# New costs for the interleaving of u products with routing and gates, and a second search over 64 pairs

## The chip, the cores and the metric

One core of a Trainium2 chip runs the whole program. The metric is device time in microseconds (us). Five engines work side by side: PE multiplies matrices (PEld is its loading of weights), DVE and POOL work on vectors, ACT computes functions and copies with a change of type, SP issues most of the DMAs. Each engine takes its own instructions strictly in the order in which the program holds them; an instruction that waits holds back all that stand behind it on its engine.

## The reference

The program has two layers on 256 tokens of width 1024. Each layer is a mixer (s5 in the first, sparse attention in the second) and then an expert layer, and the change touches the expert layers alone. Cut to what matters:

```python
qk = (h @ w_q).reshape(b, s, 8, 2, 128)              # 8 heads, two halves each
sc = einsum('bshcd,hckd->bshck', qk, sub_keys)       # 128 keys in each half
s1, i1 = top_k(sc[..., 0, :], 16)
s2, i2 = top_k(sc[..., 1, :], 16)
cand = (s1[..., :, None] + s2[..., None, :])         # 16 x 16 sums of a head
top_s, top_pos = top_k(cand.reshape(..., 256), 16)   # 16 experts of a head
gates = softmax(top_s)
act = gelu(einsum('cd,ced->ce', h, u_tab[experts])) * gates
out = einsum('ce,ced->cd', act, v_tab[experts])
```

## The kernel before

No expert is gathered. The kernel multiplies h with all 128x128 rows of u, takes the gelu, multiplies by a dense table of gates (zero where an expert was not chosen) and multiplies with all rows of v. Activations stand transposed: features or experts on the partitions, the 256 tokens along the free axis. B, one buffer of 128 x 128 x 256, holds the activations of all experts of a layer.

A product of full precision is three matmuls: a weight is split into w_hi, written by ACT (L139), and w_lo, the rest, written by DVE (L181), in halves of 128x512 with four buffers each. A "u product" (function `U`) turns one 512 KB slab of u into 24 matmuls of 128x256 (L188, L189, L190; the last needs w_lo). 128 of them make a layer, two to a bank of PSUM; a bank leaves through ACT (gelu, L733, L736) and, where gates are there already, through a DVE product (L737).

An expert layer then has four stages, all on the same five engines:

- Route (`route_steps`): per head two products with w_q (`head`), the scores, `top16` on 128 scores four times (`topk1`) and on the 256 sums for each 128 tokens (`topk2`; L864 to L868, L907).
- Decode, twice, for 128 tokens t each: positions are turned into two indices (L920 to L923), in eight parts a comparison on DVE (L930) and a product on POOL (L932) and a sum on DVE (L935); then Exp on ACT (L938), sums, and a transposition into `slotT`.
- Gates (`G`): 64 turns q of four tokens. DVE writes two tables, oij (L761) and ohl (L764), two buffers each; PE makes eight matmuls of 128x128 into one bank (L769); DVE multiplies what is there of B with that bank (L772), ACT copies the rest (L775).
- v products (`VS`, L798): 128 turns; left-over u products and, in the first layer, steps of the second layer's modulation (`ada_steps`, L233) are dealt among them.

The order in which u products are mixed with routing, decoding and gates is set by `weave`: each step of the side work yields a pair of costs (PE, DVE) in us, each u product yields its own pair, and as long as the sum of DVE costs exceeds that of PE costs the next u product is taken. A scheduler then places instructions on each engine; in decoding and among v products DVE's order is that of the code. The numbers yielded are therefore what sets the order.

Of the kernel before, what the change touches and what calls it, by code (L numbers as in the profile page):

```python
# [10 lines left out]
F16 = mybir.dt.float16  # L11
I32 = mybir.dt.int32
U32 = mybir.dt.uint32
# [697 lines left out]
def peer_layer(K, layer, h):  # L711
    tc, nc = K.tc, K.nc
    V = nc.vector
    with tc.tile_pool(name=f"pr{layer}", bufs=1, reuse_waits="tile") as pp, \
            tc.tile_pool(name=f"pw{layer}", bufs=2, reuse_waits="tile") as wp, ExitStack() as es:

        B = pp.tile([P, NJ, S], F32, name="B")
        slotT = pp.tile([P, 2, S // 2, 2, 2], F16, name="slotT")
        done = [0]
        ugelu = [0]  # L720
        u_src, v_src = K.aps["peer_u"], K.aps["peer_v"]

        def U():

            late = []

            def evac():
                c, ps = late.pop()
                pv = ps.rearrange("p (j t) -> p j t", j=2)
                t0 = done[0]  # L730
                out = B[:, 2 * c:2 * c + 2]
                if t0 < S:
                    nc.scalar.activation(out[:, :, t0:], pv[:, :, t0:], AF.Gelu_apprx_tanh)  # L733
                if t0 > 0:
                    g = wp.tile([P, 2, S], F32, name="ge", bufs=1)
                    nc.scalar.activation(g[:, :, :t0], pv[:, :, :t0], AF.Gelu_apprx_tanh)  # L736
                    V.tensor_mul(out[:, :, :t0], g[:, :, :t0], out[:, :, :t0])  # L737
                ugelu[0] = 2 * c + 2
                return 0.6 if t0 else 0.0

            for c in range(NJ // 2):
                ps = bank(K)
                for m in range(2):
                    chunk_T(K, split_w(K, load_unit(K, u_src[layer, 2 * c + m])), h, ps[:, m * S:(m + 1) * S])
                    dve = evac() if late and m == 0 else 0.0
                    yield 2.62, U_DVE + dve
                late.append((c, ps))
            evac()
            yield 0.0, 0.6

        def G(gp):

            tab = K.iota2
            full = [P, 4, P, 2]
            for q in range(S // 4):
                ts = slice(4 * q, 4 * q + 4)

                oij, ohl = (gp.tile([P, 2, 2, P, 2], F16, name=n) for n in ("oij", "ohl"))
                si, sg = (slotT[:, n, 2 * q:2 * q + 2].rearrange("p a n t -> p (a n) t")[:, :, None, :].to_broadcast(full)
                          for n in range(2))  # L760
                V.tensor_tensor(oij.rearrange("p a n j t -> p (a n) j t"), tab[:, None].to_broadcast(full), si,  # L761
                                op=OP.is_equal)
                oj = oij[:, :, 1, None].to_broadcast([P, 2, 2, P, 2])
                V.tensor_tensor(ohl, oj, slotT[:, 1, 2 * q:2 * q + 2, :, None, :].to_broadcast([P, 2, 2, P, 2]), op=OP.mult)  # L764
                ps = bank(K)
                pv = ps.rearrange("p (j t) -> p j t", t=4)
                for t in range(4):
                    for n in range(2):
                        nc.tensor.matmul(pv[:, :, t], oij[:, t // 2, 0, :, t % 2], ohl[:, t // 2, n, :, t % 2],  # L769
                                         start=(n == 0), stop=(n == 1), skip_group_check=True)  # L770
                jd = ugelu[0]
                V.scalar_tensor_tensor(B[:, :jd, ts], pv[:, :jd], 1.0 / GS, B[:, :jd, ts],  # L772
                                       op0=OP.mult, op1=OP.mult)
                if jd < NJ:
                    nc.scalar.activation(B[:, jd:, ts], pv[:, jd:], AF.Copy, scale=1.0 / GS)  # L775
                done[0] = 4 * q + 4
                yield 0.5, 1.5

        u = U()
        weave(u, route_steps(K, layer, h, B, slotT))  # L780
        assert ugelu[0] <= ROUTE_J
        with tc.tile_pool(name=f"pg{layer}", bufs=2, reuse_waits="tile") as gp:
            weave(u, G(gp))
        acc = [[bank(K) for _ in range(2)] for _ in range(2)]

        vp = es.enter_context(tc.tile_pool(name=f"pv{layer}", bufs=2, reuse_waits="tile"))

        def VS():

            for j in range(NJ):  # L790
                raw = load_unit(K, v_src[layer, j])
                with tc.high_priority(offset=PRIO):
                    a = split(K, B[:, j], [P, S], "a", pool=vp)
                for dh, w in enumerate(split_w(K, raw)):
                    for t in range(2):
                        ts = slice(t * P, (t + 1) * P)
                        for al, wl in ((0, 0), (0, 1), (1, 0)):
                            nc.tensor.matmul(acc[t][dh], a[al][:, ts], w[wl],  # L798
                                             start=(j == 0 and al + wl == 0), stop=(j == NJ - 1 and al == 1))
                yield j  # L800

        ada = ada_steps(K, vp, ADA_T) if layer == 0 else iter(())
        with tc.manual_schedule(engines={mybir.EngineType.DVE, mybir.EngineType.SP}):
            credit = 0.0
            for j in VS():
                credit += 0.4 if next(u, None) is None else 0.8
                while credit >= 1.0:
                    next(ada, None)
                    credit -= 1.0
        assert next(u, None) is None  # L810
        for _ in ada:
            pass
    return acc
# [25 lines left out]


ROUTE_J = 64
U_DVE = 1.3


def route_steps(K, layer, h, B, slotT):
# [6 lines left out]
    qk = [cv([S]) for _ in range(4)]  # L852
    sc = [cv([2, 2, P]) for _ in range(3)]
    sc2 = [cv([P]) for _ in range(2)]
    cand = [cv([16, 16]) for _ in range(2)]
    cand2 = [cv([256]) for _ in range(2)]
    val = cv([2, H, 2, TK])
    idx = cv([2, H, 2, TK], U32)
    idf = cv([2, H, 2, TK])
    ts = cv([2, H, TK])  # L860
    pos = cv([2, H, TK], U32)

    def top16(v, i, src, tmp):
        V.max(v[:, 0:8], src)  # L864
# [15 lines left out]
    def head(u):  # L880
# [4 lines left out]
        for c in range(2):  # L885
# [7 lines left out]
            while len(late) > (3 if 2 * u + c < 3 else 0):  # L893
                scores()
            late.append((u, c, q, ps2))
            yield 2.8, 1.14

    def topk1(u):
        for c in range(2):
            for t in range(2):  # L900
                top16(val[:, t, u, c], idx[:, t, u, c], sc[u % 3][:, c, t], sc2[t])
                yield 0, 1.0

    def topk2(u):
        for t in range(2):
            cd = cand[t]
            V.tensor_add(cd, val[:, t, u, 0, :, None].to_broadcast([P, 16, 16]),  # L907
                         val[:, t, u, 1, None, :].to_broadcast([P, 16, 16]))
            top16(ts[:, t, u], pos[:, t, u], cd.rearrange("p a b -> p (a b)"), cand2[t])
            yield 0, 2.0  # L910

    def decode(t):
        cw = Carve(B.rearrange("p j t -> p (j t)"), ROUTE_J * S + t * 8192)
        ab = cw([2, H, TK], U32)
        abf = cw([2, H, TK])
        sel = cw([2, H, TK])
        eq = cw([2, H, TK, 16])
        e, z, el = cw([H, TK]), cw([H]), cw([H, TK])
        e16 = cw([H * TK // 2]).bitcast(F16).rearrange("p (h k) -> p h k", h=H)
        V.tensor_scalar(ab[:, 0], pos[:, t], 4, None, op0=OP.logical_shift_right)  # L920
        V.tensor_scalar(ab[:, 1], pos[:, t], 15, None, op0=OP.bitwise_and)
        V.tensor_copy(abf, ab)
        V.tensor_copy(idf[:, t], idx[:, t])  # L923
        yield 0, 1.2
        shape = [P, 2, TK, 16]
        parts = [(c, slice(2 * i, 2 * i + 2)) for i in range(4) for c in range(2)]
        for n in range(len(parts) + 2):
            if n < len(parts):
                c, hs = parts[n]
                V.tensor_tensor(eq[:, c, hs], abf[:, c, hs, :, None].to_broadcast(shape),  # L930
                                K.iota[:, None, None, 0:16].to_broadcast(shape), op=OP.is_equal)
                nc.gpsimd.tensor_mul(eq[:, c, hs], eq[:, c, hs], idf[:, t, hs, c, None, :].to_broadcast(shape))  # L932
            if n > 1:
                c, hs = parts[n - 2]
                V.tensor_reduce(sel[:, c, hs], eq[:, c, hs], axis=AX.X, op=OP.add)  # L935
            yield 0, 1.2
        V.tensor_sub(e, ts[:, t], ts[:, t, :, 0:1].to_broadcast([P, H, TK]))
        nc.scalar.activation(e, e, AF.Exp)  # L938
        V.tensor_reduce(z, e, axis=AX.X, op=OP.add)
        V.reciprocal(z, z)  # L940
        V.scalar_tensor_tensor(e, e, GS, z[:, :, None].to_broadcast([P, H, TK]), op0=OP.mult, op1=OP.mult)
# [12 lines left out]
    for u in range(9):  # L954
# [5 lines left out]
        if u > 0:  # L960
            yield from topk1(u - 1)
            yield from topk2(u - 1)
    with K.tc.manual_schedule(engines={mybir.EngineType.DVE}):
        for t in range(2):
            yield from decode(t)

# [450 lines left out]
```

## Time and profile before

| what | us |
|---|---|
| median of 3 runs | 2086.83 |
| lowest, highest | 2086.11, 2086.85 |
| profiled execution | 2087.91 |
| its span | 2086.1 |
| PE busy in the span | 2022.8 (97%) |
| DVE busy in the span | 1609.8 (77%) |
| ACT busy in the span | 1154.2 (55%) |
| POOL busy in the span | 113.6 (5%) |

The mean granted clock of TensorE is 0.986 of full speed. In time, the first layer routes from about 212 to 345 us, decodes to 416, makes gates to 657 and v products to 1046; the second layer routes from 1240 to 1369, decodes to 1440, makes gates to 1680 and v products to 2070. A busy share is an average over these stages, so a stage has to be looked at by itself; a matmul's end is modelled, and a matmul that overlaps the one before it counts once.

### The profile page before, as it was taken

What the parts mean: (1) busy time and instruction counts of PE and PEld (TensorE: products, weight loads), DVE (VectorE), ACT (ScalarE), POOL (GpSimd) and SP (SyncE); (2) the same over time, 40 slices, a digit from 0 to 9 for tenths busy, and PEclk for the clock granted to TensorE, in tenths of its full rate; (3) what the DMA queues carried; (4) which work ended last, traced back from release to release, by engine and by line L of the source; (5) the groups of instructions that cost most, each with busy time, mean ns of one, the idle gap of its engine ahead of it and who ended that gap; (6) DMA issues with size and microseconds to landing.
All of it is one profiled execution on the core that took longest, in us unless ns stands there. A gap on an engine that the chain in (4) does not pass through costs nothing. (4 is left out here: it accounts for less than half of the span.)

```text
span 2086.1 us, 39288 instructions
## 1 busy us (share of the span) xinstructions
PE 2022.8 (97%) x14344; PEld 1840.6 (88%) x14344; DVE 1609.8 (77%) x3698; ACT 1154.2 (55%) x2396; POOL 113.6 (5%) x149
## 2 busy tenths in 40 slices
PE   6889999999999999999999999999999999999998
PEld 3778999899999988888888789999999998888887
DVE  9696899878887777777775869998788865556665
ACT  4775555555445555555555755555554455555554
POOL 4220001200000000000010000021000000000000
PEclk9899999999999999999999999999999999999998
DMA  7445555544445788888863045555444455666562
GB/s 285 147 180 162 162 172 172 157 151 139 142 142 177 259 277 267 271 268 270 276 228 112 22 141 163 172 165 163 138 142 142 142 173 189 194 192 193 193 195 95
DMA packets 102690, 377.18 MB, mean 181 GB/s; under 512 B 11488, under 2 KB 11872, under 8 KB 101472
## 3 DMA queue, kind: packets, MB, share of 16 engines
q1 hardware_dynamic: 101520, 371.42, 55.1%
q0 software_dynamic: 544, 2.61, 0.4%
q8 instruction: 112, 1.84, 0.4%
q14 instruction: 82, 0.67, 0.1%
q10 hardware_dynamic: 432, 0.65, 0.1%
HBM read 373.07 MB, written 1.05 MB: 179 GB/s over the span
## 5 line engine op out<-in xcount | busy, mean ns | idle before, releaser
L139 ACT ACTIVATE w_hi<-raw 128x512 fp32r<-128x512 f32 x1194 | 746.5, 628 | 733.5 <-PE bank L189 432.2
L181 DVE TENSOR_TENSOR w_lo<-raw,w_hi 128x512 fp32r<-128x512 f32 x1194 | 815.6, 704 | 131.5 <-ACT w_hi L139 129.6
L188 PE MATMUL bank<-h_hi,w_hi 128*128 128x256 f32 x2504 | 717.3, 289 | 9.0 <-ACT w_hi L139 5.7
L190 PE MATMUL bank<-h_hi,w_lo 128*128 128x256 f32 x2504 | 709.4, 286 | 11.7 <-DVE w_lo L181 11.7
L189 PE MATMUL bank<-h_lo,w_hi 128*128 128x256 f32 x2504 | 709.8, 285 | 1.4 <-DVE h_lo L304 1.4
L188 PEld LDWEIGHTS bank<-h_hi,w_hi 128*128 128x128 f32 x2504 | 485.5, 195 | 17.2 <-ACT w_hi L139 8.3
L190 PEld LDWEIGHTS bank<-h_hi,w_lo 128*128 128x128 f32 x2504 | 480.7, 193 | 16.3 <-DVE w_lo L181 15.7
L189 PEld LDWEIGHTS bank<-h_lo,w_hi 128*128 128x128 f32 x2504 | 483.4, 193 | 3.8 <-DVE h_lo L304 2.7
L798 PE MATMUL bank<-w_lo,a_hi 128*128 128x512 f32 x1024 | 398.8, 389 | 0.2 <-DVE w_lo L181 0.2
L798 PE MATMUL bank<-w_hi,a_lo 128*128 128x512 f32 x1024 | 398.5, 389 | 0.0
L798 PE MATMUL bank<-w_hi,a_hi 128*128 128x512 f32 x1024 | 281.0, 389 | 0.0
L181 DVE TENSOR_TENSOR a_lo<-B,a_hi 128x256 fp32r<-128x256 f32 x256 | 108.7, 425 | 197.9 <-ACT a_hi L139 197.8
L798 PEld LDWEIGHTS bank<-w_hi,a_lo 128*128 128x128 f32 x1024 | 192.2, 188 | 40.0
L798 PEld LDWEIGHTS bank<-w_lo,a_hi 128*128 128x128 f32 x1024 | 192.3, 188 | 39.7 <-DVE w_lo L181 0.7
L798 PEld LDWEIGHTS bank<-w_hi,a_hi 128*128 128x128 f32 x1024 | 191.4, 188 | 38.5
L769 PE MATMUL bank<-ohl,oij 128*128 128x128 f16 x1024 | 129.2, 307 | 0.0
L139 ACT ACTIVATE a_hi<-B 128x256 fp32r<-128x256 f32 x256 | 106.8, 418 | 27.0 <-PE bank L798 14.4
L772 DVE SCALAR_TENSOR_TENSOR B<-bank,B 128x216 f32<-128x216 f32 (+31 forms) x128 | 62.6, 489 | 71.9 <-PE bank L769 71.1
L769 PEld LDWEIGHTS <-oij 128*128 128x128 f16 x1024 | 101.5, 128 | 4.2
L761 DVE TENSOR_TENSOR oij<-iota,slotT 128x1024 f16<-128x1024 f16 x128 | 89.3, 699 | 0.0
L764 DVE TENSOR_TENSOR ohl<-oij,slotT 128x1024 f16<-128x1024 f16 x128 | 88.9, 695 | 0.1
L233 DVE SCALAR_TENSOR_TENSOR raw<-raw,cb 128x1024 f32<-128x1024 f32 x56 | 68.3, 1219 | 0.0
(261 smaller groups left out, 1758.6 us busy)
## 6 DMA issues: line engine op xcount, KB each, us to landing
raw<-peer_u SPq DMA_DIRECT2D x256, 512.0 KB, 3.6
raw<-peer_v SPq DMA_DIRECT2D x256, 512.0 KB, 4.0
raw<-ada_t SPq DMA_DIRECT2D x56, 512.0 KB, 4.6
raw<-ada_w SPq DMA_DIRECT2D x40, 512.0 KB, 5.2
raw<-w_q SPq DMA_DIRECT2D x32, 512.0 KB, 3.6
raw<-w_glu SPq DMA_DIRECT2D x16, 512.0 KB, 4.4
raw<-w_in SPq DMA_DIRECT2D x8, 512.0 KB, 6.1
w<-w_cmp SPq DMA_DIRECT2D x4, 1024.0 KB, 9.3
```

Source lines behind the costliest of these rows:

```text
L139: nc.scalar.activation(hi, raw, AF.Copy)
L181: K.nc.vector.tensor_tensor(lo, raw, hi.bitcast(F32), op=OP.subtract)
L188: nc.tensor.matmul(out, wh, xh, start=start, stop=False)
L189: nc.tensor.matmul(out, wh, xl, start=False, stop=False)
L190: nc.tensor.matmul(out, wl, xh, start=False, stop=stop)
L233: V.scalar_tensor_tensor(w, w, 1.0, cb, op0=OP.mult, op1=OP.mult, accum_out=part[:, m:m + 1])
L761: V.tensor_tensor(oij.rearrange("p a n j t -> p (a n) j t"), tab[:, None].to_broadcast(full), si, op=OP.is_equal)
L764: V.tensor_tensor(ohl, oj, slotT[:, 1, 2 * q:2 * q + 2, :, None, :].to_broadcast([P, 2, 2, P, 2]), op=OP.mult)
L769: nc.tensor.matmul(pv[:, :, t], oij[:, t // 2, 0, :, t % 2], ohl[:, t // 2, n, :, t % 2], start=(n == 0), stop=(n == 1), skip_group_check= ...
L772: V.scalar_tensor_tensor(B[:, :jd, ts], pv[:, :jd], 1.0 / GS, B[:, :jd, ts], op0=OP.mult, op1=OP.mult)
L798: nc.tensor.matmul(acc[t][dh], a[al][:, ts], w[wl], start=(j == 0 and al + wl == 0), stop=(j == NJ - 1 and al == 1))
```

## The change

Every cost that `weave` reads is set anew: a u product from (2.62, 1.3) to (2.87, 1.43), a turn of gates from (0.5, 1.5) to (0.87, 1.85), a step of `head` from (2.8, 1.14) to (2.87, 1.43), `topk1` from 1.0 to 1.65, `topk2` from 2.0 to 1.75, decoding from 1.2 to 1.4 a step. The second search looks at 64 of the 256 pairs, among which the 16 largest sums of two sorted lists must lie. The decoding of positions is done once for both halves (`places`, 14 DVE instructions on 256 or 512 elements), and both Exp stand ahead of it (`weights`).

```diff
-                    yield 2.62, U_DVE + dve
+                    yield 2.87, U_DVE + dve
...
-                yield 0.5, 1.5
+                yield 0.87, 1.85
...
-U_DVE = 1.3
+U_DVE = 1.43
+CAND = ((0, 1, 16), (1, 3, 8), (4, 4, 4), (8, 8, 1))
+NCAND = 64
...
-            yield 2.8, 1.14
+            yield 2.87, 1.43
...
-                yield 0, 1.0
+                yield 0, 1.65
...
+        at = 0
+        for a0, na, nb in CAND:
+            shape = [P, 2, na, nb]
+            V.tensor_tensor(cand[:, :, at:at + na * nb].rearrange("p t (a b) -> p t a b", a=na),
+                            val[:, :, u, 0, a0:a0 + na, None].to_broadcast(shape),
+                            val[:, :, u, 1, None, 0:nb].to_broadcast(shape), op=OP.add)
+            at += na * nb
         for t in range(2):
-            cd = cand[t]
-            V.tensor_add(cd, val[:, t, u, 0, :, None].to_broadcast([P, 16, 16]),
-                         val[:, t, u, 1, None, :].to_broadcast([P, 16, 16]))
-            top16(ts[:, t, u], pos[:, t, u], cd.rearrange("p a b -> p (a b)"), cand2[t])
-            yield 0, 2.0
+            top16(ts[:, t, u], pos[:, t, u], cand[:, t], cand2[t])
+            yield 0, 1.75
+
+    def places():
...
+        V.tensor_scalar(sh[:, 0], p2, 3, None, op0=OP.logical_shift_right)
+        V.tensor_scalar(sh[:, 1], p2, 2, None, op0=OP.logical_shift_right)
+        V.tensor_copy(f, sh)
+        V.tensor_copy(pf, p2)
+        V.tensor_copy(idf, idx)
+        yield 0, 1.6
...
+        yield 0, 1.2
...
+        yield 0, 2.2
+
+    def weights():
+        for t in range(2):
...
+            V.tensor_sub(w["e"], ts[:, t], ts[:, t, :, 0:1].to_broadcast([P, H, TK]))
+            nc.scalar.activation(w["e"], w["e"], AF.Exp)
 
     def decode(t):
...
-        V.tensor_copy(idf[:, t], idx[:, t])
-        yield 0, 1.2
...
-            yield 0, 1.2
-        V.tensor_sub(e, ts[:, t], ts[:, t, :, 0:1].to_broadcast([P, H, TK]))
-        nc.scalar.activation(e, e, AF.Exp)
+            yield 0, 1.4
...
     with K.tc.manual_schedule(engines={mybir.EngineType.DVE}):
+        weights()
+        yield from places()
         for t in range(2):
             yield from decode(t)
```

Where the order moves, first on DVE in the gate stage. A bank is the PSUM bank of one turn q, an ohl is the second table of one turn. Before, at turns 11 and 12 (banks 6025 and 6040); ohl_6125 is of turn 13, whose bank is 6128, and ohl_6140 of turn 14:

```order
L772 SCALAR_TENSOR_TENSOR B_2696<-bank_6025,B_2696 128x60x4
L761 TENSOR_TENSOR oij_6124<-iota2_71,slotT_2697 128x1024
L181 TENSOR_TENSOR w_lo_6097<-raw_6090,w_hi_6096 128x512
L772 SCALAR_TENSOR_TENSOR B_2696<-bank_6040,B_2696 128x60x4
L761 TENSOR_TENSOR oij_6139<-iota2_71,slotT_2697 128x1024
L764 TENSOR_TENSOR ohl_6125<-oij_6124,slotT_2697 128x1024
L181 TENSOR_TENSOR w_lo_6158<-raw_6155,w_hi_6157 128x512
L764 TENSOR_TENSOR ohl_6140<-oij_6139,slotT_2697 128x1024
L737 TENSOR_TENSOR B_2696<-ge_6087,B_2696 128x2x52
L181 TENSOR_TENSOR w_lo_6162<-raw_6155,w_hi_6161 128x512
L181 TENSOR_TENSOR w_lo_6211<-raw_6208,w_hi_6210 128x512
L772 SCALAR_TENSOR_TENSOR B_2696<-bank_6128,B_2696 128x62x4
```

After, at turns 11, 12 and 13 (banks 6500, 6549, 6564); ohl_6561 is of turn 13 and ohl_6649 of turn 14:

```order
L772 SCALAR_TENSOR_TENSOR B_2696<-bank_6500,B_2696 128x74x4
L761 TENSOR_TENSOR oij_6560<-iota2_71,slotT_2697 128x1024
L772 SCALAR_TENSOR_TENSOR B_2696<-bank_6549,B_2696 128x74x4
L761 TENSOR_TENSOR oij_6648<-iota2_71,slotT_2697 128x1024
L181 TENSOR_TENSOR w_lo_6621<-raw_6614,w_hi_6620 128x512
L764 TENSOR_TENSOR ohl_6561<-oij_6560,slotT_2697 128x1024
L764 TENSOR_TENSOR ohl_6649<-oij_6648,slotT_2697 128x1024
L772 SCALAR_TENSOR_TENSOR B_2696<-bank_6564,B_2696 128x74x4
```

Before, both tables of the next two turns are written behind the two products of the turns before them, and PE has 48 matmuls of u products to do meanwhile. After, the table of turn 13 (ohl_6561) is written behind the product of turn 12 (L772 of bank 6549), the first table of turn 14 and a w_lo.

Second, on PE at the same turns, with the semaphores that an instruction waits for. Before, from the last u matmuls ahead of turn 13 into its first gate matmuls:

```order
L190 MATMUL bank_6051<-h_hi_2662,w_lo_6097 128x256
L188 MATMUL bank_6051<-h_hi_2662,w_hi_6096 128x256
L189 MATMUL bank_6051<-h_lo_2663,w_hi_6096 128x256
L190 MATMUL bank_6051<-h_hi_2662,w_lo_6097 128x256
L769 LDWEIGHTS oij_6124 [waits DVE_49]
L769 MATMUL bank_6128<-ohl_6125,oij_6124 128x128 [waits PE_49]
L769 LDWEIGHTS oij_6124
L769 MATMUL bank_6128<-ohl_6125,oij_6124 128x128
```

After, from the last gate matmuls of turn 12 (bank 6549) into those of turn 13 (bank 6564):

```order
L769 LDWEIGHTS oij_6545
L769 MATMUL bank_6549<-ohl_6546,oij_6545 128x128
L769 LDWEIGHTS oij_6545
L769 MATMUL bank_6549<-ohl_6546,oij_6545 128x128
L769 LDWEIGHTS oij_6560 [waits DVE_49]
L769 MATMUL bank_6564<-ohl_6561,oij_6560 128x128 [waits PE_49]
L769 LDWEIGHTS oij_6560
L769 MATMUL bank_6564<-ohl_6561,oij_6560 128x128
```

Before, 48 u matmuls stand between turn 12 and turn 13. After, the weights of turn 13 are loaded right behind the matmuls of turn 12, with a wait for DVE. In the order after there are seven such turns in each layer (the 13th, 20th, 27th, 34th, 41st, 48th and 57th, counted from 0), where the ohl of a turn stands behind the L772 of the turn before it on DVE and no u matmul stands between the two turns on PE; in five of the seven a w_lo is on the way as well. The order before has none. The u products still to do when the gates end are 9 instead of 15, and in the order after the first v matmuls follow the last turn's gate matmuls directly, where two u products stood between them before.

Third, on DVE from the end of the first decode into the second. Before:

```order
L937 TENSOR_TENSOR B<-B 128x128
L939 TENSOR_REDUCE B<-B 128x8
L940 RECIPROCAL B<-B 128x8
L941 SCALAR_TENSOR_TENSOR B<-B 128x128
L944 TENSOR_TENSOR B<-B 128x128
L920 TENSOR_SCALAR B<-B 128x128
L921 TENSOR_SCALAR B<-B 128x128
L922 CAST B<-B 128x256
L923 CAST B<-B 128x256
L181 TENSOR_TENSOR w_lo<-raw,w_hi 128x512 x2
L930 TENSOR_TENSOR B<-B,cst 128x512
```

After:

```order
L979 TENSOR_REDUCE B<-B 128x8
L980 RECIPROCAL B<-B 128x8
L981 SCALAR_TENSOR_TENSOR B<-B 128x128
L984 TENSOR_TENSOR B<-B 128x128
L972 TENSOR_TENSOR B<-B,cst 128x512
L181 TENSOR_TENSOR w_lo<-raw,w_hi 128x512 x2
```

The subtraction ahead of Exp (L937) and the four instructions on positions (L920 to L923) are gone from here; the lines L979 to L984 are the sums of L939 to L944, L972 is L930.

## Rows read from the trace of the kernel before

**Rows 1.** Busy time by stretch: us, then PE, PEld, DVE, ACT, POOL, PEclk, DMA share, GB/s.
```profile
240.00:344.00 104.00, 104.00 (x872) 104.00 (x872) 102.64 (x403) 55.48 (x97) 0.00 (x0) 1.00 0.56 178
344.00:380.00 36.00, 34.15 (x277) 33.17 (x275) 31.95 (x53) 19.57 (x33) 10.95 (x8) 1.00 0.52 162
380.00:420.00 40.00, 36.29 (x292) 35.21 (x293) 37.42 (x59) 21.66 (x40) 11.12 (x8) 1.00 0.51 153
425.00:640.00 215.00, 215.00 (x1836) 213.02 (x1834) 176.33 (x319) 105.32 (x230) 0.00 (x0) 1.00 0.45 140
1366.00:1404.00 38.00, 36.30 (x295) 35.30 (x293) 33.95 (x61) 20.73 (x34) 10.95 (x8) 1.00 0.53 166
1404.00:1445.00 41.00, 37.17 (x300) 36.09 (x301) 37.88 (x61) 22.42 (x41) 11.14 (x8) 1.00 0.51 156
```

**Rows 2.** Costliest groups, by form, in 240 to 340: search on 256 candidates.
```profile
L867 DVE MAX8 B<-B 128x8 f32<-128x256 f32 x12 | 5.1, 425 | 0.0
```

**Rows 3.** Timeline of DVE, first decode: start us, us, engine, line, operation [idle before].
```profile
358.56 0.68 DVE L930 TENSOR_TENSOR B<-B,cst 128x512 f32<-128x512 f32 x1
...
359.76 2.00 DVE L181 TENSOR_TENSOR w_lo<-raw,w_hi 128x512 fp32r<-128x512 f32 x2
361.69 0.68 DVE L930 TENSOR_TENSOR B<-B,cst 128x512 f32<-128x512 f32 x1
...
377.13 0.29 DVE L939 TENSOR_REDUCE B<-B 128x8 f32<-128x128 f32 x1 [2.17 <-ACT B L938]
...
379.76 0.29 DVE L944 TENSOR_TENSOR B<-B 128x128 f32<-128x128 f32 x1 [1.77 <-ACT B L942]
```

**Rows 4.** Timeline of DVE, second decode: the first gate tables among the steps.
```profile
385.49 2.38 DVE L761 TENSOR_TENSOR oij<-iota,slotT 128x1024 f16<-128x1024 f16 x2
```

**Rows 5.** Timeline of PE in the gate stage: one group of eight, then two groups.
```profile
586.05 1.05 PE L769 MATMUL bank<-ohl,oij 128*128 128x128 f16 x8
...
461.29 1.92 PE L769 MATMUL bank<-ohl,oij 128*128 128x128 f16 x16
462.97 0.36 PE L188 MATMUL bank<-h_hi,w_hi 128*128 128x256 f32 x1
```

**Rows 6.** Timeline of DVE at that one group.
```profile
587.14 0.55 DVE L772 SCALAR_TENSOR_TENSOR B<-bank,B 128x376 f32<-128x376 f32 x1 [0.36 <-PE bank L769]
587.61 0.68 DVE L761 TENSOR_TENSOR oij<-iota,slotT 128x1024 f16<-128x1024 f16 x1
588.20 0.68 DVE L181 TENSOR_TENSOR w_lo<-raw,w_hi 128x512 fp32r<-128x512 f32 x1
588.81 0.68 DVE L764 TENSOR_TENSOR ohl<-oij,slotT 128x1024 f16<-128x1024 f16 x1
```

**Rows 7.** Costliest groups of DVE, by form, in 440 to 640: the narrower gate product.
```profile
L772 DVE SCALAR_TENSOR_TENSOR B<-bank,B 128x296 f32<-128x296 f32 x2 | 0.9, 468 | 1.5 <-PE bank L769 1.5
```

**Rows 8.** Costliest groups of the whole page: the ACT part of a v product.
```profile
L139 ACT ACTIVATE a_hi<-B 128x256 fp32r<-128x256 f32 x256 | 106.8, 418 | 27.0 <-PE bank L798 14.4
```

**Rows 9.** Timeline of DVE at the end of the first layer's v products.
```profile
1041.78 0.42 DVE L181 TENSOR_TENSOR a_lo<-B,a_hi 128x256 fp32r<-128x256 f32 x1 [1.09 <-ACT a_hi L139]
...
1043.40 1.22 DVE L233 SCALAR_TENSOR_TENSOR raw<-raw,cb 128x1024 f32<-128x1024 f32 x1
```

**Rows 10.** Timeline of PE: waits of three lengths in the first stage.
```profile
71.01 0.58 PE L188 MATMUL bank<-h_hi,w_hi 128*128 128x256 f32 x1 [3.81 <-ACT w_hi L139]
...
99.98 0.39 PE L188 MATMUL bank<-h_hi,w_hi 128*128 128x256 f32 x1 [1.86 <-ACT w_hi L139]
...
122.07 1.14 PE L617 MATMUL bank<-rH,wo 128*32 128x63 f32 x51 [1.81 <-DVE rH L602]
```

**Rows 11.** Busy time by stretch, right behind those three waits.
```profile
72.00:76.00 4.00, 4.00 (x18) 3.82 (x18) 3.39 (x8) 0.00 (x0) 1.38 (x2) 0.50 0.67 230
102.00:106.00 4.00, 4.00 (x26) 4.00 (x25) 3.99 (x9) 2.99 (x7) 1.71 (x3) 0.64 0.54 188
120.00:124.00 4.00, 2.17 (x73) 1.78 (x73) 4.00 (x12) 3.90 (x12) 0.26 (x1) 1.00 0.97 391
```

More of the change, by code (lines that the diff above doesn't have):

```diff
@@ L854, in route_steps @@
     sc2 = [cv([P]) for _ in range(2)]
-    cand = [cv([16, 16]) for _ in range(2)]
-    cand2 = [cv([256]) for _ in range(2)]
+    cand = cv([2, NCAND])
+    cand2 = [cv([NCAND]) for _ in range(2)]
     val = cv([2, H, 2, TK])
@@ L861, in route_steps @@
     pos = cv([2, H, TK], U32)
+    ab = cv([2, 2, H, TK])
+    assert cv.at == ROUTE_J * S + 7680
     def top16(v, i, src, tmp):
@@ L901, in topk1 @@
                 top16(val[:, t, u, c], idx[:, t, u, c], sc[u % 3][:, c, t], sc2[t])
-                yield 0, 1.0
+                yield 0, 1.65
     def topk2(u):
-        for t in range(2):
-            cd = cand[t]
-            V.tensor_add(cd, val[:, t, u, 0, :, None].to_broadcast([P, 16, 16]),
-                         val[:, t, u, 1, None, :].to_broadcast([P, 16, 16]))
-            top16(ts[:, t, u], pos[:, t, u], cd.rearrange("p a b -> p (a b)"), cand2[t])
-            yield 0, 2.0
-    def decode(t):
[L913 to L922, printed above, removed]
-        V.tensor_copy(idf[:, t], idx[:, t])
-        yield 0, 1.2
+        at = 0
@@ new lines, in topk2 @@
+        for a0, na, nb in CAND:
[4 more added lines that the diff above has]
+            at += na * nb
+        for t in range(2):
+            top16(ts[:, t, u], pos[:, t, u], cand[:, t], cand2[t])
+            yield 0, 1.75
+    def places():
+        cw = Carve(B.rearrange("p j t -> p (j t)"), ROUTE_J * S + 12360)
+        sh = cw([2, 256], U32)
+        pf, m, n = cw([256]), cw([256]), cw([256])
+        f = cw([2, 256])
+        p2 = pos.rearrange("p t h k -> p (t h k)")
+        a, b = (ab[:, :, c] for c in range(2))
+        v = lambda x: x.rearrange("p (t h k) -> p t h k", t=2, h=H)
+        V.tensor_scalar(sh[:, 0], p2, 3, None, op0=OP.logical_shift_right)
[4 more added lines that the diff above has]
+        yield 0, 1.6
+        V.tensor_scalar(m, f[:, 0], -1.0, 0.0, op0=OP.add, op1=OP.max)
+        V.scalar_tensor_tensor(m, f[:, 1], -6.0, m, op0=OP.add, op1=OP.max)
+        V.scalar_tensor_tensor(a, v(pf), -48.0, v(m), op0=OP.add, op1=OP.max)
+        yield 0, 1.2
+        V.tensor_scalar(v(m), a, 8.0, 8.0, op0=OP.mult, op1=OP.add)
+        V.scalar_tensor_tensor(v(m), a, 16.0, v(m), op0=OP.mult, op1=OP.min)
+        V.tensor_scalar(v(n), a, 4.0, 24.0, op0=OP.mult, op1=OP.add)
+        V.tensor_tensor(m, m, n, op=OP.min)
+        V.scalar_tensor_tensor(v(m), a, 48.0, v(m), op0=OP.add, op1=OP.min)
+        V.tensor_sub(b, v(pf), v(m))
+        yield 0, 2.2
@@ new lines, in route_steps @@
+    ws = []
+    def weights():
+        for t in range(2):
+            cw = Carve(B.rearrange("p j t -> p (j t)"), ROUTE_J * S + t * 7680)
+            w = dict(sel=cw([2, H, TK]), eq=cw([2, H, TK, 16]), e=cw([H, TK]), z=cw([H]), el=cw([H, TK]),
+                     e16=cw([H * TK // 2]).bitcast(F16).rearrange("p (h k) -> p h k", h=H))
+            ws.append(w)
+            V.tensor_sub(w["e"], ts[:, t], ts[:, t, :, 0:1].to_broadcast([P, H, TK]))
+            nc.scalar.activation(w["e"], w["e"], AF.Exp)
@@ L925, in decode @@
+    def decode(t):
+        sel, eq, e, z, el, e16 = (ws[t][n] for n in ("sel", "eq", "e", "z", "el", "e16"))
         shape = [P, 2, TK, 16]
@@ L929, in decode @@
                 c, hs = parts[n]
-                V.tensor_tensor(eq[:, c, hs], abf[:, c, hs, :, None].to_broadcast(shape),
+                V.tensor_tensor(eq[:, c, hs], ab[:, t, c, hs, :, None].to_broadcast(shape),
                                 K.iota[:, None, None, 0:16].to_broadcast(shape), op=OP.is_equal)
```

## The prediction

> **What bounds the kernel now.** I read the busy time by stretch first. In routing and in the gate stage PE is busy all the time at full clock (104.00 of 104.00 us, 215.00 of 215.00), while DVE has 102.64 us of work in the first stretch and 176.33 in the second [rows 1]. There time is lost only if PE is made to wait. In decoding PE is not full. The same rows give the size: in routing 872 matmuls take 104.00 us, 0.1193 us each, so a u product of 24 takes 2.86 us. By that pitch the 277, 292, 295 and 300 matmuls of the four decoding stretches are 33.0, 34.8, 35.2 and 35.8 us of work in 36, 40, 38 and 41 us: 3.0 + 5.2 + 2.8 + 5.2 = 16.2 us in which PE stood still. That is all that the change can win in decoding. The timeline of DVE says why: one step of decoding (start of L930 to start of the next L930) takes 3.13 us with two w_lo in it, which take 2.00 [rows 3], so a product of 2.86 us comes 0.27 us late; and at the end of a decode DVE waits 2.17 and 1.77 us for ACT and makes no w_lo meanwhile [rows 3].
>
> Weighed against that: by PE's busy time the same four stretches lose 1.85, 3.71, 1.70 and 3.83 us, together 11.1; by the weight loads' busy time 15.2 [rows 1]. The Trainium skill, "Trainium Kernel Development and Optimization" (Best Practices), says that the distance of TensorE from its limit is to be judged by the busy share of weight loads, not of matmuls. The trace agrees: 15.2 stands beside the 16.2 by count, and by matmul busy time the win below would be about 5 us smaller.
>
> **The change part by part.**
>
> Search on 64 pairs. It takes work off DVE: an instruction on 256 candidates takes 425 ns [rows 2], on 64 between nothing and that. No row shows one on 64, and it does not matter: PE has no idle time in routing to give back. Could DVE be late there instead? The new costs place about 15 more u products per layer ahead of the gates (64 instead of 49, counted in the order). They bring PE 15 x 2.86 = 42.9 us, and DVE two w_lo each at the 0.60 us from start to start [rows 6], 18 us. The same search is spread over more PE time, so routing stays at the pace of PE: 0. The products moved there are gone from the later stages, whose pace is PE's too. SP issues their loads in the same order; 178 GB/s at a DMA share of 0.56 [rows 1] leaves room.
>
> Decoding. Work on positions: 14 DVE instructions for both halves, no row of theirs on these sizes; bounds are nothing and the 0.67 us that 128x512 takes on DVE, near the 0.29 of the smaller ones [rows 3], say 4.2 us in all. Beside them stand four u products (11.4 us of PE, 4.8 us of w_lo), so they hide, and PE's buffer of w_lo is full behind them with some 2.4 us to spare. That carries the first decode's eight steps (8 x 0.27 = 2.2 us). Exp no longer ends a wait; ACT has 19.57 of 36 us busy there [rows 1], so the two early Exp hide. What stays late is the second decode: the wait for the cast (1.77 us [rows 3]), two oij (2.30 of the 2.38 us [rows 4]), two ohl (1.2) and four later steps (1.1), 6.4 us, against a lead of some 3.3 us from the steps without a sum or without a comparison. I keep 3.1 us a layer, 6.2 for both. Win: 16.2 - 6.2 = 10.0 us. Bounds: 16 (nothing stays), 5 (the second decode and its tail lose what they lost).
>
> Gates: the term that decides. A gate turn is now priced nearer to PE's cost, so fewer u products are dealt into it: about 55 for 64 turns, 0.86 each. Seven times a layer a turn comes directly behind another on PE, and the order shows what its tables wait for. Take turn 12 and 13. Turn 13's weight load waits for ohl on DVE; ohl stands behind L772 of turn 12, which waits for PE's own eight matmuls of turn 12, then an oij and a w_lo. This is a loop through both engines with nothing on PE in between. Its length from rows, counted from the first matmul of turn 12:
> - L772 starts 587.14 - 586.05 = 1.09 us later [rows 5, 6].
> - It holds DVE for its pitch. At 376 elements that is 587.61 - 587.14 = 0.47 with a duration of 0.55 [rows 6], so 0.08 less than the duration. At 296 elements 0.468 - 0.08 = 0.39 [rows 7]; by these two 0.0010 us an element, so 0.51 at 416 and 0.55 at 448.
> - oij 0.59 to 0.60, w_lo 0.61, from start to start; ohl 0.68 to its end [rows 6].
> - PE's own work: 16 gate matmuls take 462.97 - 461.29 = 1.68 us, a turn 0.84 [rows 5].
> At turn 13: 1.09 + 0.39 + 0.60 + 0.61 + 0.68 - 0.84 = 2.53 us of PE standing still. The five turns with a w_lo (296 to 392 elements) give 2.53 to 2.63, together 12.9; the two without (416 and 448) 2.04 and 2.08, together 4.1. That is 17.0 us a layer, 34.0 for both. Behind the waiting load stand all of PE's matmuls, 48 of u products first, which need nothing of DVE by then; L772 of the turn and ACT's copy wait for PE. Nothing is won back: before and after, PE is the engine that this stage waits for. The bounds are 2.0 and 2.7 a turn (28 and 38), and zero if the loop does not bind (a rival below).
>
> From gates to v products. The first v matmuls now follow turn 63 directly, and need its L772 and then ACT's copy of an activation, 418 ns [rows 8]: 1.09 + about 0.60 + 0.42 - 0.84 = 1.3 us a layer, 2.6 for both. In the order before, two u products (5.7 us) lay over it.
>
> The modulation's steps. Fewer left-over u products (9, not 15) earn the first layer's v products less credit, so three steps L233 of 1.22 us stand in a row ahead of one a_lo near their end. DVE has 1.09 us free in a turn [rows 9]. 0.5 us; bounds 0 and 1.2.
>
> Sum: -10.0 + 34.0 + 2.6 + 0.5 = +27.1. The profiled execution took 2087.91 us (span 2086.1) and the median is 2086.83, 1.1 lower; durations carry over, so 2086.8 + 27.1 = 2113.9 us. Its own range, from the bounds: stalls 28 to 38, win 16 to 5: 2102 to 2123.
>
> **The rivals.**
>
> The clock falls at the stalls. A wait of 3.81 us, at 71.01, was followed by a stretch at half clock (0.50 in 72 to 76); one of 1.81, at 122.07, lies in a stretch at 1.00; one of 1.86, at 99.98, amid sparse work, was followed by 0.64 in 102 to 106 [rows 10, 11]. The new stalls of 2.1 to 2.6 lie between. For it: the 1.86. Against it: ahead of 99.98 PE was far from full, and in the gates it works without a gap up to the stall. Price: 4 us at 0.50 lose 2.0, at 0.64 lose 1.4; 14 times 20 to 28 more, 2134 to 2142 us. Beside it stands the Trainium skill, "TensorE: Matmul & The Clock Gate" (HAM oscillation — how this bites in real kernels): short bursts of matmuls, each ended by a wait, bring the clock down at every one of them. No row here shows such a repeated fall within the expert layers.
>
> Decoding is not relieved. If w_lo stays at 2.00 a pair in all steps and the lead of the first decode is used up early, the win is 0 to 5 instead of 10: 2119 to 2124. For it: POOL's products, which run beside (10.95 us in 36 [rows 1]), are the same. Against it: the two waits for ACT at the end shrink in any case.
>
> The other side: the loop does not bind. Pairs of turns stand back to back before as well (16 gate matmuls in a row at 461.29 [rows 5]) with no wait between them. If ohl were there in time at the 14 places too, the time is 2086.8 - 10.0 + 2.6 + 0.5 = 2079.9, faster. The point from which it decides: below (10.0 - 3.1) / 14 = 0.49 us a stall. Against it: in the old pairs both ohl stand ahead of the first turn's L772, and in the new places the second one stands behind it.
>
> **How the numbers follow.** The forecast, 2113.9, has 0.67; the clock 0.15; decoding not relieved 0.10; the loop not binding 0.06; stalls and win that cancel 0.02. The range 2105 to 2138 leaves out the faster and equal cases (0.08), the lowest part of the forecast's own range and the highest of the clock's. Measurement can tell about 0.2% (4 us) from no change: faster 0.06, within 0.02, slower 0.92.
>
> **What would show it.** In the gate stage: 14 waits on PE at L769, ended by ohl (L764), of 2.0 to 2.7 us, about 34 us together, and PE less than full in 425 to 640. The granted clock there tells the second rival. In decoding: no wait for Exp on DVE, and PE's waits for w_lo of L190 cut by more than half. At the first v matmul a wait of about 1.3 us. The prediction is wrong if these waits are under 0.5 us each, or if PE's idle time turns up in routing, where DVE would then be late.

## The result

| | before | after |
|---|---|---|
| median, us (runs) | 2086.51 (6) | 2137.43 (6) |
| lowest, highest | 2086.11, 2088.25 | 2135.49, 2139.17 |
| profiled span | 2086.1 | 2134.2 |
| mean granted clock | 0.986 | 0.978 |

The change makes the kernel slower: ratio 1.0242, 95% interval 1.0229 to 1.0255, or +50.9 us where +27.1 was forecast (2113.9, range 2105 to 2138).

The waits of PE over the whole span are the first view. Each line says which PE line waited for what, then total us, times, longest. After:

```profile
PE bank L769 <- DVE ohl L764: 35.1, 14, 2.8
PE bank L798 <- ACT a_hi L139: 4.1, 2, 2.9
PE bank L190 <- DVE w_lo L181: 3.8, 7, 1.0
```

Before, the same view has no line for L769 or for a_hi, and these two:

```profile
PE bank L190 <- DVE w_lo L181: 11.7, 16, 1.4
PE bank L947 <- DVE B L944: 0.6, 2, 0.3
```

The 14 new waits are there, and the waits of decoding are cut by two thirds. The difference of these lines is +30.7 us, though, and the span grew by 48.1. The gate stage of the first layer shows what else. The columns of the busy time by stretch are those of [rows 1]:

```profile
450.00:690.00 240.00, 222.44 (x1829) 218.72 (x1828) 184.08 (x323) 101.77 (x230) 0.00 (x0) 0.96 0.38 122
```

PE is 17.6 us short of full, just the sum of this layer's seven waits, where it was full before, and the clock is 0.96 instead of 1.00 [rows 1]. Here are the first of the waits on PE and, below it, the loop on DVE:

```profile
496.48 1.05 PE L769 MATMUL bank<-ohl,oij 128*128 128x128 f16 x8
499.89 1.89 PE L769 MATMUL bank<-ohl,oij 128*128 128x128 f16 x8 [2.36 <-DVE ohl L764]
```

```profile
497.57 0.47 DVE L772 SCALAR_TENSOR_TENSOR B<-bank,B 128x296 f32<-128x296 f32 x1 [0.41 <-PE bank L769]
497.95 0.68 DVE L761 TENSOR_TENSOR oij<-iota,slotT 128x1024 f16<-128x1024 f16 x1
498.55 0.69 DVE L181 TENSOR_TENSOR w_lo<-raw,w_hi 128x512 fp32r<-128x512 f32 x1
499.15 1.29 DVE L764 TENSOR_TENSOR ohl<-oij,slotT 128x1024 f16<-128x1024 f16 x2
```

L772 starts 1.09 us after turn 12's first matmul, just as in [rows 5, 6], and oij, w_lo and ohl follow as the order said. The eight matmuls behind the wait take 1.89 us instead of 1.05. That is the clock, and a wait of nearly the same length in the same place of the second layer is not followed by it. The 4 us behind a wait of 2.41 us (at 554.73), behind one of 2.36 (at 1552.66) and behind one of 2.78 (at 671.43):

```profile
554.73:558.73 4.00, 4.00 (x23) 4.00 (x24) 2.56 (x5) 0.51 (x2) 0.00 (x0) 0.63 0.47 135
1552.66:1556.66 4.00, 4.00 (x35) 4.00 (x36) 3.09 (x6) 1.09 (x3) 0.00 (x0) 1.00 0.36 131
671.43:675.43 4.00, 4.00 (x35) 3.96 (x36) 3.46 (x6) 0.95 (x3) 0.00 (x0) 1.00 0.24 89
```

23 matmuls instead of 35 in 4 us: this fall to the lower level (1.2 instead of 2.4 GHz) costs 4 x 0.37 = 1.5 us. In this profile the clock fell behind 9 of the 14 waits of L769, at 1.5 to 1.7 us each and 14.5 us together, and behind the first wait for a_hi (1.6 us): ten times in all, 16 us. (The expectations below speak of ten falls in the gates; there were nine, and the tenth at the first v product.)

Decoding, against the four stretches of [rows 1]:

```profile
372.00:448.00 76.00, 74.71 (x610) 73.27 (x608) 72.43 (x117) 41.81 (x71) 22.12 (x16) 1.00 0.55 172
1432.00:1510.00 78.00, 76.71 (x628) 75.24 (x627) 72.28 (x107) 41.53 (x72) 22.14 (x16) 1.00 0.57 177
```

610 and 628 matmuls of 0.1193 us are 72.8 and 74.9 us: PE stands still for 3.2 and 3.1 us, 6.3 in both layers instead of 16.2. The sum is closed with the waits counted as the prediction counted them, from the last issue and not from the modelled end of the last matmul (499.89 - 496.48 - 0.84 = 2.57 where the profile writes 2.36): 35.1 + 14 x 0.21 = 38.0; 38.0 - 9.9 + 4.1 + 16 = 48.2 of 48.1. It closes better than it should: the sum has no term for the way from the first layer's last v matmul to the next layer's norm (L279), which takes 11.0 us instead of 8.0, so about 2 us are counted too much elsewhere.

### The profile page after: what moved, and what is told of

Same layout as the page of the kernel before. It is cut to its first block, busy times and chain, and to the rows that moved or that the text cites. A ratio compares the mean times of both kernels' runs of the same rounds, so it can differ in the third digit from the quotient of the medians.

```text
span 2134.2 us, 39367 instructions
## 1 busy us (share of the span) xinstructions
PE 2038.2 (96%) x14344; PEld 1852.6 (87%) x14344; DVE 1587.2 (74%) x3726; ACT 1143.0 (54%) x2384; POOL 113.3 (5%) x149
## 3 DMA queue, kind: packets, MB, share of 16 engines
HBM read 373.07 MB, written 1.05 MB: 175 GB/s over the span
## 5 line engine op out<-in xcount | busy, mean ns | idle before, releaser
L190 PE MATMUL bank<-h_hi,w_lo 128*128 128x256 f32 x2504 | 716.3, 287 | 4.0 <-DVE w_lo L181 3.8
L190 PEld LDWEIGHTS bank<-h_hi,w_lo 128*128 128x128 f32 x2504 | 486.8, 194 | 8.2 <-DVE w_lo L181 7.4
L769 PE MATMUL bank<-ohl,oij 128*128 128x128 f16 x1024 | 135.0, 316 | 35.1 <-DVE ohl L764 35.1
L769 PEld LDWEIGHTS <-oij 128*128 128x128 f16 x1024 | 105.2, 131 | 42.7 <-DVE ohl L764 39.0
L772 DVE SCALAR_TENSOR_TENSOR B<-bank,B 128x264 f32<-128x264 f32 (+27 forms) x128 | 68.4, 534 | 76.4 <-PE bank L769 75.8
L775 ACT ACTIVATE B<-bank 128x248 f32<-128x248 f32 (+27 forms) x128 | 37.2, 291 | 78.2 <-DVE B L772 76.0
```

The source lines that it names most:

```text
L190: nc.tensor.matmul(out, wl, xh, start=False, stop=stop)
```

## The experiments

Theory A: the loop through PE and DVE at 14 turns and the clock's falls behind its waits make the loss; decoding wins by itself. Rivals: the clock falls because the work is denser; DVE is late anyway; code and costs only act together.

**One price back.** The gate turn's price alone, at 1.62 for DVE where it was 1.5 before the change; it deals about one u product to each turn.

```diff
-                yield 0.87, 1.85
+                yield 0.5, 1.62
```

> The changed kernel with one number back: a gate turn is priced (0.5, 1.62), which deals about one u product to each turn again; routing and decoding stay as changed. In its order no turn's ohl stands behind the product of the turn before it without 24 matmuls between. Theory A (the loop through both engines at 14 turns, and the clock falling behind most of these waits, make up the loss): the waits of L769 for ohl go from 35.1 us to under 1, the gates run at full clock, and the decode keeps its win of 10. Now no u product is left for the v products, so their credit is 51.2 instead of 54.8, and some six L233 of 1.2 us stand behind the last v product (0 to 7 us); the first v product still follows the gates directly (4 us and a fall of the clock). Time 2083 to 2092 us. Theory B (the clock falls because routing and gates are denser, not because of the waits): falls stay, some 17 us more, 2100 to 2109.

Measured: 2092.53 us, ratio 1.0027 (1.0016 to 1.0038). L769 waits for nothing, and the same stretch of the gate stage reads:

```profile
450.00:690.00 240.00, 240.00 (x2049) 237.75 (x2048) 195.82 (x346) 115.75 (x257) 0.00 (x0) 1.00 0.46 143
```

PE full, clock full, 220 more matmuls in the same 240 us. That price carries 45 of the 51 us. Routing is as dense as in the change and the gates are denser, so density does not bring the clock down. The time lies half a microsecond above the expected band; of what is left, two waits of PE speak, and the way from the first layer's last v matmul to the next norm, which takes 15.2 us here:

```profile
PE bank L798 <- ACT a_hi L139: 5.5, 2, 4.4
PE bank L833 <- ACT o L826: 2.8, 1, 2.8
```

**Extra work in the hole.** Matmuls that do nothing where PE waits.

```diff
+                if q in (13, 20, 27, 34, 41, 48, 57):
+                    for _ in range(18):
+                        nc.tensor.matmul(ps[:, :S], h[0][:, 0, :P], h[0][:, 0], start=True, stop=True,
+                                         skip_group_check=True)
```

> The changed kernel with 18 extra matmuls of 128x256 on PE at each of the seven turns of a layer where PE waits for ohl (252 in all, 0.119 us each, 30 us of PE), written into the turn's own bank ahead of the gate matmuls, which overwrite them. They do nothing for the output. Theory A: PE's idle time there is replaced by nearly as much work, so waits of L769 fall from 35 to under 5 us, and the clock stays full in the gates: 2137.4 - 35 + 30 + 3 - 16.5 (ten falls of 1.65) = 2116 to 2122 us. Theory B (the clock falls for another reason): 2132 to 2138. Theory C (PE is throttled by dense work): slower than 2138.

Measured: 2119.88 us, ratio 1.0158 (1.0141 to 1.0175): 17.6 us faster than the change, with 252 matmuls more. In this order 23 to 32 u matmuls also came to stand behind the extra ones at each of the 14 places, 2.7 to 3.8 us of work and thus more than the wait there. So the run takes the waits away and adds 30 us of PE's time; it does not show that the extra matmuls alone would have filled the holes. The whole stage, in the change and then here, and PE's waits here:

```profile
425.00:690.00 265.00, 246.15 (x2014) 241.25 (x2013) 208.00 (x360) 113.82 (x250) 6.48 (x5) 0.97 0.39 126
425.00:690.00 265.00, 259.76 (x2188) 255.63 (x2187) 211.36 (x365) 118.85 (x260) 6.49 (x5) 1.00 0.42 128
```

```profile
PE bank L773 <- DVE ohl L764: 2.0, 4, 0.8
```

The granted clock is 1.00 over the stage (0.97 in the change). PE's time spent on nothing is nearly the same: 35.1 us of waits there, 2.0 of waits and 30 of extra work here, 3 us less (5 by the count from the last issue). The other 12 to 15 us of the 17.6 are the clock's part, and the nine falls of the gates lost 14.5 by their rows. This separates the two: the waits cost 35 to 38 us, the falls they bring some 15.

**The tables first.** Dealing unchanged, oij and ohl with priority on DVE.

```diff
-                V.tensor_tensor(oij.rearrange("p a n j t -> p (a n) j t"), tab[:, None].to_broadcast(full), si,
+                with tc.high_priority(offset=PRIO):
+                    V.tensor_tensor(oij.rearrange("p a n j t -> p (a n) j t"), tab[:, None].to_broadcast(full), si,
...
-                V.tensor_tensor(ohl, oj, slotT[:, 1, 2 * q:2 * q + 2, :, None, :].to_broadcast([P, 2, 2, P, 2]), op=OP.mult)
+                    V.tensor_tensor(ohl, oj, slotT[:, 1, 2 * q:2 * q + 2, :, None, :].to_broadcast([P, 2, 2, P, 2]), op=OP.mult)
```

> The changed kernel, with the two tables of a gate turn (oij, ohl) given priority on DVE; the dealing of u products is unchanged, so the seven back-to-back turns of a layer are still there. In its order ohl stands ahead of the earlier turn's product at four of the seven; at three (41, 48, 57) it stands right behind it, without the oij and the w_lo between. Theory A: eight waits vanish and six shrink to 1.09 + 0.5 + 0.68 - 0.84 = 1.4 us: L769 waits 8 to 10 us in place of 35, with few or no falls of the clock: 2094 to 2104 us. Rival (DVE is late in the gates anyway, and the time moves to waits of L190 for w_lo): 2125 to 2137.

Measured: 2106.16 us, ratio 1.0091 (1.0074 to 1.0108), 31 us faster than the change; the waits of L190 stay at 3.9. So with the same dealing the order on DVE decides over these 31 us, and DVE had the time. But the waits left are larger than expected, 17.5 us in eight instead of 8 to 10 in six:

```profile
PE bank L770 <- DVE ohl L765: 17.5, 8, 2.8
```

The timeline of PE shows the shortest, at turn 34, where none was expected, and a long one, at turn 48; DVE at each of them stands below:

```profile
568.68 1.05 PE L770 MATMUL bank<-ohl,oij 128*128 128x128 f16 x8 [1.39 <-DVE ohl L765]
...
620.43 1.05 PE L770 MATMUL bank<-ohl,oij 128*128 128x128 f16 x8 [2.71 <-DVE ohl L765]
```

```profile
566.21 0.69 DVE L762 TENSOR_TENSOR oij<-iota,slotT 128x1024 f16<-128x1024 f16 x1 [0.80 <-PE bank L770]
566.81 0.53 DVE L773 SCALAR_TENSOR_TENSOR B<-bank,B 128x368 f32<-128x368 f32 x1
567.33 0.69 DVE L762 TENSOR_TENSOR oij<-iota,slotT 128x1024 f16<-128x1024 f16 x1
567.94 0.68 DVE L765 TENSOR_TENSOR ohl<-oij,slotT 128x1024 f16<-128x1024 f16 x1
...
617.49 0.58 DVE L773 SCALAR_TENSOR_TENSOR B<-bank,B 128x416 f32<-128x416 f32 x1
618.00 0.68 DVE L181 TENSOR_TENSOR w_lo<-raw,w_hi 128x512 fp32r<-128x512 f32 x1
618.59 0.68 DVE L762 TENSOR_TENSOR oij<-iota,slotT 128x1024 f16<-128x1024 f16 x1
619.20 0.58 DVE L773 SCALAR_TENSOR_TENSOR B<-bank,B 128x416 f32<-128x416 f32 x1
619.70 1.28 DVE L765 TENSOR_TENSOR ohl<-oij,slotT 128x1024 f16<-128x1024 f16 x2
```

At turn 34 ohl does stand ahead of the product of the turn before, but the oij it needs starts only when PE is done with turn 32: it reads nothing of PE's, so it waits for one of its two buffers, and a product and another oij follow ahead of ohl. At turn 41 (1.86 us) an oij still stands ahead of the product. At turns 48 and 57 three turns stand in a row on PE: DVE must first finish the product of the first of them, a w_lo and an oij before it gets to the product of the second, and these waits are as long as in the change (2.71 and 2.78). The estimate had let that product start at once. Waits of 1.39 and 1.86 us left the clock at full here; of the four long ones, the two of the first layer brought it down.

**The code with the old costs.** Every cost of before in the changed code; the steps of `places`, which the code of before has not, keep theirs.

```diff
-                    yield 2.87, U_DVE + dve
+                    yield 2.62, U_DVE + dve
-                yield 0.87, 1.85
+                yield 0.5, 1.5
-U_DVE = 1.43
+U_DVE = 1.3
...
```

> The changed code (64 pairs, positions decoded once, both Exp ahead) with every cost of before. In its order no turn waits in the loop and two u products stand between gates and v products, as before. Theory A (the costs alone bring the loss, and the code alone or with the u products dealt to decoding brings the win): waits of L190 for w_lo go from 11.7 to 4 to 8 us, nothing else moves: 2077 to 2083 us. Rival (the win in decoding needs the new costs, which put 15 more u products ahead of the gates): 2085 to 2088.

Measured: 2080.82 us, ratio 0.9969 (0.9957 to 0.9982), faster than before by 5.8 us (3.8 to 9.0). PE's waits for w_lo:

```profile
PE bank L190 <- DVE w_lo L181: 3.8, 7, 1.0
```

As in the change, with 15 fewer u products ahead of the gates. The win in decoding does not need the new costs.

**The costs alone.** The new numbers in the code of before.

```diff
-                    yield 2.62, U_DVE + dve
+                    yield 2.87, U_DVE + dve
-                yield 0.5, 1.5
+                yield 0.87, 1.85
...
```

> The kernel before with the new costs alone (search on 256, decoding and Exp as before). Its order has the loop at 14 turns again, at the same numbers q, at two of them (13 and 77) with L772 and ohl alone. Theory A (the costs carry the whole loss, the code wins its 6 to 10 us by itself): waits of L769 for ohl 30 to 36 us, 6 to 12 of them with the clock falling behind, waits of L190 for w_lo near those of before (8 to 12 us): 2137 to 2148 us, at least as slow as the full change. Rival (code and costs only lose together): below 2125.

Measured: 2135.85 us, ratio 1.0226 (1.0210 to 1.0241), 1.2 us under the expected band.

```profile
PE bank L769 <- DVE ohl L764: 32.6, 14, 2.8
PE bank L190 <- DVE w_lo L181: 7.8, 10, 1.9
```

The costs carry the whole loss. The waits for w_lo are smaller than before even with the old code, so part of decoding's win comes with either half of the change. The halves do not add: +48.4 us for the costs and -5.8 for the code, each against before on its own chip, and +50.9 together. With the new costs in place the code takes 4.0 us off the waits for w_lo, but the waits of the loop are 2.5 us longer with it (turn 13 waits 1.15 us here and 2.36 in the change), and the clock fell behind nine of them instead of eight.

**The credit too.** The first experiment with one more number.

```diff
-                credit += 0.4 if next(u, None) is None else 0.8
+                credit += 0.45 if next(u, None) is None else 0.8
```

> As the kernel with the gate turn's price put back (2092.5 us), and the credit of a v turn without a u product is 0.45 instead of 0.4, so that the modulation's steps are done within the v products. Theory A (of its 6 us over the kernel before, most is the steps that stood behind the last v product, and the wait for the first v product stays): the waits of L833 and L260 at the end of the first layer's v products go back, 2084 to 2088 us. Rival (the 6 us are the first v product's wait and its fall of the clock): 2091 to 2093.

Measured: 2085.71 us, ratio 0.9991 (0.9982 to 1.0000): 6.8 us off, as theory A has it. L833 waits no more, and the way from the last v matmul to the next norm takes 8.2 us instead of 15.2. The time is still 4.9 us above the code with the old costs (2080.8), and the waits for the first v products, which that one does not have, are 5.5 us here as in the first experiment, with a fall of the clock behind the longer one.

**Exp ahead alone.** One part of the code in the kernel before.

```diff
-        V.tensor_sub(e, ts[:, t], ts[:, t, :, 0:1].to_broadcast([P, H, TK]))
-        nc.scalar.activation(e, e, AF.Exp)
...
     with K.tc.manual_schedule(engines={mybir.EngineType.DVE}):
+        weights()
```

> The kernel before with one part of the change: both subtractions and both Exp stand ahead of the decoding; search, positions and costs are those of before. Theory A (the win of decoding is mostly the waits of DVE for ACT at each decode's end, 2.2 and 1.8 us in the first, and the table load between): waits of L190 for w_lo go from 11.7 to 5 to 8 us: 2081 to 2084.5 us. Rival (the win is the shared decoding of positions and the smaller search): 2085.5 to 2087.

Measured: 2080.57 us, ratio 0.9964 (0.9950 to 0.9977), half a microsecond below the expected band. DVE at the end of the first decode, where it waited 1.77 us for ACT before [rows 3], and PE's waits:

```profile
376.85 0.29 DVE L947 TENSOR_TENSOR B<-B 128x128 f32<-128x128 f32 x1 [0.38 <-ACT B L945]
```

```profile
PE bank L190 <- DVE w_lo L181: 6.0, 8, 1.7
```

The wait for Exp is gone, and the one for the cast behind it shrank by 1.39 us as well, which no step of the prediction had (ACT's table load behind Exp takes 1.28 us; it was not tried by itself). This part alone gives what the whole code gives with the old costs (-6.9 and -5.8 us, each against before on its own chip); the 64 pairs and the shared positions take 2.2 us off the waits for w_lo, which the time doesn't show.

**The change again.** A second profile of the same kernel.

> The changed kernel once more, for a second profile. Theory A (where the clock falls is not set by the length of a wait): the same 14 waits of L769, 35 us together, each within 0.1 us of its length in the first profile, and the clock falls behind other ones of them than before; the time goes with the number of falls, 1.65 us each. Rival (the longer waits, or fixed places, bring it down): the same ten.

Measured: one time, 2139.32 us (span 2137.5). The waits of L769 are 35.1 us in 14 again, each of the same length. The clock fell behind ten of them, and not the same ones; behind the wait of 2.41 (at 554.90) and the one of 2.36 (at 1554.38) it is the other way round than in the first profile:

```profile
554.90:558.90 4.00, 4.00 (x34) 4.00 (x35) 3.26 (x6) 1.04 (x3) 0.00 (x0) 1.00 0.45 135
1554.38:1558.38 4.00, 4.00 (x21) 4.00 (x22) 2.40 (x5) 0.35 (x1) 0.00 (x0) 0.57 0.40 131
671.79:675.79 4.00, 4.00 (x35) 3.96 (x36) 3.46 (x6) 0.96 (x3) 0.00 (x0) 1.00 0.27 104
```

So neither the length of such a wait nor its place in the program settles it, and what does stays open. The wait of 2.78 left the clock alone in both profiles, but one of 2.76 did not in the kernel with the costs alone, nor one of 2.78 with the tables first. One fall more explains 1.7 of the 3.3 us between the two spans; the rest lies outside the gates.

## Why the prediction was right in kind and short in size

The direction, the place and the loop as the cause were right. The time itself was not: 2137.4 us lies above the forecast's own range (2102 to 2123), and within the stated one only because that took in most of the rival of the falling clock, with 0.6 us to spare. That much is luck. In the rival's band of 2134 to 2142 us the time lies by a sum that is not the rival's: fewer falls, longer waits.

**The loop: right.** 14 waits, at the turns named, ended by ohl, 35.1 us (38.0 counted from the last issue) where 34.0 was forecast. The five of a layer with a w_lo were 2.57 by that count at turn 13, forecast 2.53; at the two others the forecast was short. At turns 48 and 57 the profile writes 2.71 and 2.78 where 2.04 and 2.08 were forecast: the term "L772 starts 1.09 us later" fails there, because turn 47 itself stands directly behind turn 46 and DVE has that turn's product, an oij and a w_lo to do first. That is nearly all of the 4 us by which the waits exceed the forecast.

**The clock: the step that failed.** It stood among the rivals with 0.15, because PE works without a gap up to each stall. That was no protection: 9 falls behind 14 waits in one profile, 10 in the other, 1.5 to 1.7 us each. The rival's price of 1.4 to 2.0 was right, its count of 14 too high, and its chance far too low; measured and forecast differ by 23.5 us, and this is 16 of them, the fall at the first v product included. In the loop that the Trainium skill tells of there ("TensorE: Matmul & The Clock Gate", HAM oscillation — how this bites in real kernels) the clock is down after every wait, and these are waits of 3 to 5 us; the waits here are shorter, and the traces show two in three.

**Decoding: right as a sum, partly wrong in its parts.** 9.9 us won by the count, 10.0 forecast. The prediction kept 1.77 us for the wait for the cast; it fell to 0.38 in the change too (at 415.77). PE waits for no w_lo in the first decode of either layer; the longest wait left is 0.96 us (at 430.00), in the second decode right behind the first gate tables, as the prediction had it. That the search on 64 pairs is worth nothing while PE is full fits the runs: Exp ahead alone gives as much as the whole code, search and shared positions together.

**From gates to v products: the place right, the price too low.** 2.6 us forecast, 4.1 measured and a fall of the clock (1.6). The second layer has 1.2 of them; in the first, ACT has the start of the modulation's steps in front of a_hi, a table load among it, as its timeline shows (no run moved them):

```profile
695.23 1.28 ACT L226 ACT_TABLE_LOAD   x1
696.52 1.06 ACT L226 ACTIVATE cb<-raw 128x1024 f32<-128x1024 f32 x1
697.49 0.71 ACT L139 ACTIVATE a_hi<-B 128x256 fp32r<-128x256 f32 x2
```

ACT's queue ahead of the waiting instruction was not looked at.

**The modulation's steps: the price too low.** They were forecast at 0.5 us, at most 1.2, near the end of the first layer's v products. No v matmul waits for DVE there, but behind the last one the way to the next norm takes 11.0 us instead of 8.0. The sums of squares (L260) stand on it, and the clock falls earlier than before. Here are the same two microseconds behind the last v matmul (5.5 to 7.5 us), first before, then after, and below them the matmuls of L260, 32 in each kernel:

```profile
1052.00:1054.00 2.00, 1.16 (x11) 1.08 (x10) 0.29 (x2) 1.81 (x3) 0.00 (x0) 0.94 1.01 409
1077.00:1079.00 2.00, 2.00 (x11) 2.00 (x11) 0.25 (x1) 0.92 (x3) 0.00 (x0) 0.50 1.03 359
```

```profile
1048.91 1.05 PE L260 MATMUL bank<-ones,sq 128*128 128x1 f32 x8
1050.30 2.87 PE L260 MATMUL bank<-ones,sq 128*128 128x1 f32 x24 [0.33 <-ACT sq L249]
...
1075.39 6.00 PE L260 MATMUL bank<-ones,sq 128*128 128x1 f32 x32 [0.94 <-ACT sq L249]
```

That these steps can do this is shown by the two kernels with the gate price back (15.2 us with steps left over, 8.2 with none); for the change itself it was not tried.

**The other rivals.** Decoding was relieved, and the loop bound everywhere it was expected to.

## What to carry to other kernels

Truer costs for dealing work do not by themselves make a better schedule: a slightly larger share of "filler" work per turn kept PE busy across a round trip through DVE, and a price nearer to PE's own cost took the filler away at seven turns of a layer. Before new costs are accepted, look in the order for two neighbours on the bottleneck engine where the second needs something that stands behind the first one's result on another engine. Count a stall of TensorE as long as these (2.4 us and more) as its length plus a share of a fall of the clock, and when a change has two halves, run them apart: the useful part here was a subtraction and an Exp of each decode, moved forward.

## What the runs showed of the hardware

In otherwise dense work at 2.4 GHz, waits of TensorE in the gate stage of 2.36 to 2.78 us brought it to 1.2 GHz in about two cases of three (29 of 44, in three kernels, one of them profiled twice), for 1.4 to 1.7 us each, and not at the same waits from one profile to the next. The wait of 2.93 us at the first v product did in all five profiles that have it. Waits of 1.15, 1.39 and 1.86 us (two of each) did not in the gate stage; the one of 1.86 us in sparse work [rows 10, 11] stands beside a clock of 0.64. Where the order left no such wait in the gates (the price back, the extra matmuls), the clock stayed at full there.
